# Duplicated keys, fewer threshold counts on one engine, and the value products of attention taken head by head

## The chip, the cores and the metric

The kernel runs on one core of a Trainium2 chip. The core has TensorE (PE; its weight loads are listed apart as PEld), VectorE (DVE), ScalarE (ACT), GpSimd (POOL) and SyncE (SP, which here only issues transfers). The metric is the device time of one execution in microseconds (us).

## The reference, cut to what matters

One layer of a hybrid encoder: 1024 prompt frames and 32 sample frames go through an input projection; its columns feed an indexer with sparse attention (eight query heads, four key/value heads) and an RWKV-7 recurrence; then an output projection and a squared-ReLU MLP follow.

```python
dots = jnp.einsum('bthd,bsd->bths', qi, ki_all) * (IDX_DIM ** -0.5)
score = jnp.einsum('bths,bth->bts', jax.nn.relu(dots), wi)
score = jnp.where(admissible[None], score, -jnp.inf)
_, idx = lax.top_k(score, topk)                       # topk = 256 for the prompt, 136 for the sample
...
s = jnp.einsum('btkgd,btskd->btkgs', qg, kg) * (HEAD_DIM ** -0.5)
p = jax.nn.softmax(jnp.where(valid[:, :, None, None, :], s, -jnp.inf), axis=-1)
o = jnp.einsum('btkgs,btskd->btkgd', p, vg)
...
y = h + jnp.square(jax.nn.relu(rms_norm(h) @ w_ff1)) @ w_ff2
```

## The kernel before

Frames go in nine tiles: t = 0 to 7 are 128 prompt frames each (tile t sees 128(t+1) keys), t = 8 is the 32 sample frames (544 keys). Products that need accuracy split an operand in a high part (F32R) and the remainder. The order of the instructions on each engine is laid down when the program is built: the code emits work in program order with priorities, and a planner with its own costs places it. So a line may run well ahead of or behind its place in the code.

**Index scores** (`idx_tile`, called for the tiles in the order 2, 3, 4, 5, 8, 6, 7). For each of eight index heads and each piece of up to 512 keys, line 324 multiplies the stacked query (high part on rows 0 to 63, remainder on rows 64 to 127) with the high part of the keys, which stands twice (`kiA`, 128 rows); line 325 adds the product of the high query with the remainder of the keys (`kiB`, 64 rows). ACT takes the relu (326), DVE weighs and sums (330). The projections of other tiles (209) run between them.

**Threshold search** (`topk`). The 256th largest score of each row is found bit by bit in 31 steps: count the scores below a candidate, then three small DVE instructions (365, 366, 368) set the next candidate. There are two groups of tiles (`SLS`). Group 0, tiles 2, 3, 4, 5, 8, counts on DVE (341). Group 1, tiles 6 and 7, counts on ACT (363), but in the first 15 steps (`i >= 16`) it too counts on DVE, since those steps of both groups read `S.upper`, copies of the upper halves of the scores as bf16, which ACT makes in `main2` (519). `norm_tile` calls and `zs_block` calls (three fills of 24 products of 352 columns in line 441, from which ACT writes `zm` and `tm`, 450 and 451; DVE copies two columns to `shl`, 446) each end with one step of both groups. PE has two buffers for these fills.

**Attention** (`attn_all`) and the **recurrence** (`rwkv_all`) run interleaved, as two generators; the recurrence has a front (with the triangular inverse, `lane_inverse`, DVE 832, 843 and POOL 837, 839) and a back per 256 frames. Attention goes through 36 items: four key/value heads j, and for each the nine tiles (8, 0, 1, 2, 3, 4, 5, 7, 6), two query heads per item. `prep` transposes the keys (1070) and splits them in `Ks` or `Kp`, with the high part on rows 0 to 63 and the remainder on rows 64 to 127; `query` puts the high query twice in `Q` (1093, 1094) and its remainder in `Ql` (1095, 64 rows). `scores` multiplies `Q` (1107, 128 rows) and `Ql` (1108, 64 rows). `turn` transposes the exponentials (1131). `product` multiplies 128 keys of values (64 features) with both heads' 256 columns at once (1146), output 64 features by 256; at the item's end it transposes the inverse sums by head (1151), multiplies (1153, 1154) and stores. After it come the output projection (1264) and the MLP (1328, 1348).

Of the kernel before, what the change touches and what calls it, by code (L numbers as in the profile page):

```python
# [150 lines left out]
def phase_a(S, pwx, pwy, pa, pi, px, xp, ps, late):  # L151
# [92 lines left out]
    S.upper = None  # L244
# [5 lines left out]
    kiB = pi.tile([64, 1024], F32R, name="kiB")  # L250
    ksA = pi.tile([128, 544], F32R, name="ksA")
    ksB = pi.tile([64, 544], F32R, name="ksB")
# [34 lines left out]
    def key_turn(t):  # L287
        r = rows_of(t)
        if t < 8:
            key_T(kiA, kiB, t * 128, KN.pop(t), r)  # L290
        else:
            key_T(ksA, ksB, 512, KN.pop(t), r)

    def cache_keys():
        for c in range(4):
            ck = pa.tile([128, 64], F32, name="ck", bufs=2)
            nc.sync.dma_start(ck, I["cache_kidx"][0, 0, c * 128:(c + 1) * 128])
            key_T(ksA, ksB, c * 128, ck, 128)

    def idx_tile(t, W):  # L300
        r = rows_of(t)
        z = pa.tile([128, 512], F32, name="zq", bufs=ZQB)[:r]
        proj_tok(z, t, W, 512)
        rope(z.rearrange("p (h d) -> p h d", h=8), t, 8)
        pt = ps.tile([128, 4, 128], F32, name="pt", bufs=2)
        for b in range(4):
            nc.tensor.transpose(pt[:, b, :r], z[:, b * 128:(b + 1) * 128], S.ident[:r, :r])
        qs = late["pj"].tile([128, 4, 2, 128], F32R, name="qs", bufs=2)
# [35 lines left out]
    def topk(X):  # L344
# [9 lines left out]
        for i in range(30, -1, -1):  # L354

            upper = i >= 16 and S.upper
            if X.exact or upper:
                count(X, ALU.is_lt, c_of, S.upper if upper else S.sc)
            else:
                for j, t in enumerate(X.SL):  # L360
                    r = rows_of(t)
                    n = S.sc[t].shape[1]
                    nc.scalar.activation(junk2[:r, :n], S.sc[t][:r, :n], AF.Sign, bias=c_of(j, r), scale=-1.0,
                                         accum_out=cnt[:r, j:j + 1])
            nc.vector.tensor_tensor(nac, cnt, X.off[:, 0] if X.exact or upper else X.off[:, 1], op=ALU.is_gt)
# [61 lines left out]
    def zs_block(i, W, o_, pool, mu1):  # L427
# [5 lines left out]
        for b, (o, n) in enumerate(TB):  # L433
# [78 lines left out]
    def main2():  # L512
        S.upper, c = {}, 0
        for X in TK:
            for t in X.SL:
                n = S.sc[t].shape[1]
                S.upper[t] = junk2 if t == 7 else S.eqb[:, c:c + n]
                c += n * (t != 7)
                (nc.gpsimd.tensor_copy if t in UPP else nc.scalar.copy)(S.upper[t][:rows_of(t), :n], S.sc[t][:rows_of(t)].bitcast(BF16)[:, 1:2 * n:2])
# [532 lines left out]
def attn_all(S, ap, ps):  # L1052
# [6 lines left out]
    def prep(j, samp):  # L1059
# [4 lines left out]
        A = ap.tile([128, n], F32R, name="K" + sx, bufs=1)  # L1064
        for t0 in range(0, nt, 4):
            t1 = min(nt, t0 + 4)
            p = ps.tile([128, 512], F32, name="ptr", bufs=PTB)
            for t in range(t0, t1):
                r = 32 if t == 4 and samp else 128
                nc.tensor.transpose(p[0:64, (t - t0) * 128:(t - t0) * 128 + r], kt[:r, t], S.ident[:r, :r])  # L1070
# [4 lines left out]
        J[j, samp] = A, vt  # L1075

    def query(k):
# [13 lines left out]
        w.Ql = Y = ap.tile([64, 2, 128], F32R, name="Ql", bufs=2)  # L1091
        src = p.rearrange("p (h q) -> p h q", h=2)[:, :, :r]
        nc.scalar.activation(X[0:64, :, :r], src, AF.Copy, scale=0.125)
        nc.scalar.activation(X[64:128, :, :r], src, AF.Copy, scale=0.125)
        nc.vector.scalar_tensor_tensor(Y[:, :, :r], src, 0.125, X[0:64, :, :r].bitcast(F32), op0=ALU.mult, op1=ALU.subtract)

    def scores(k, h):
# [3 lines left out]
        A = J[j, t == 8][0]  # L1101
        w.s[h] = s = ap.tile([128, 1024], F32, name="s", bufs=XPB)[:r, :n]
        m = w.m[:, h * 3:h * 3 + 2]
        for i, c0 in enumerate(range(0, n, 512)):
# [3 lines left out]
            nc.tensor.matmul(pd, w.Ql[:, h, :r], A[0:64, c0:c1], start=False, stop=True)  # L1108
# [26 lines left out]
    def product(k, g, nk, x, hi):  # L1135
# [3 lines left out]
        if g == 0:  # L1139
            w.pb = ps.tile([128, 512], F32, name="po", bufs=1)[0:64]  # L1140
            w.po = w.pb[:, 0:2 * r].rearrange("p (h q) -> p h q", h=2)
# [7 lines left out]
        p = w.pb[:, 256:256 + 2 * r].rearrange("p (h q) -> p h q", h=2)  # L1149
# [5 lines left out]
        nc.sync.dma_start(S.od[j * 128:j * 128 + 128, t * 128:t * 128 + r].rearrange("(h p) q -> p h q", h=2), t1)  # L1155
# [234 lines left out]
UPP = ()  # L1390
# [17 lines left out]
SLS = ((2,3,4,5,8),(6,7))  # L1408
# [11 lines left out]
def body(tc, I, O, dbg=None):  # L1420
# [4 lines left out]
    with pool(name="const") as cp, pool(name="dram", space=DRAM) as dp:  # L1425
# [18 lines left out]
        with pool(name="xnt") as xp, pool(name="psA", space=PSUM) as ps:  # L1444
# [16 lines left out]
            S.eqb = eq.rearrange("p a b -> p (a b)").bitcast(BF16)  # L1461
# [86 lines left out]
```

## Time and profile before

| | |
|---|---|
| time, three runs | 1846.62, 1850.66, 1853.6 us; median 1850.66 |
| profiled execution | 1847.36 us, span 1845.6 us |
| PE busy, share of the span | 1716.0 us, 93% |
| DVE, ACT, POOL busy | 986.4, 674.8, 587.0 us |
| chain that ended last | PE 66%, DVE 17%, POOL 6% |

A busy PE is modelled: products overlap, so busy time isn't the time that the products need. Where products follow each other without a wait, the distance from start to start tells that. The profile's chain is the work that ended last, followed back from the end; its shares tell which engine set the time of a stretch.

### The profile page before, as it was taken

Reading aid. Unit: us, or ns where it says so; the run is one execution under the profiler, and the core shown is the slowest. Engines: PE = TensorE matmul, PEld = TensorE weight load, DVE = VectorE, ACT = ScalarE, POOL = GpSimd, SP = SyncE. Lnnn points to the kernel's source line nnn. Section 1 sums busy time; section 2 is a strip of 40 time slices with the busy share of each in tenths; the row PEclk is TensorE's granted clock in tenths of the full one; section 3 lists DMA queues with packets and bytes.
Section 4 is the critical chain, followed back from the end, with each engine's and each line's share of the span. In section 5 each row is a group of like instructions: output and inputs, shape, how many; then the busy total and the mean of one; then the engine's idle time right before and its main releaser. Section 6 shows DMA issues by size and latency. Waiting matters only on the chain.

```text
span 1845.6 us, 29489 instructions
## 1 busy us (share of the span) xinstructions
PE 1716.0 (93%) x11394; PEld 1489.6 (81%) x11394; DVE 986.4 (53%) x2127; ACT 674.8 (37%) x1469; POOL 587.0 (32%) x894
## 2 busy tenths in 40 slices
PE   7999978798669988999899999999999999999999
PEld 6666667797546666666657779999999999999998
DVE  6456599999988777686552543222222222222224
ACT  6455432367635453454641332121212121212120
POOL 7446463244345434055210113121212131313120
PEclk9999988899658897999989999999999999999999
DMA  7111011132311112041212532111111111111105
GB/s 215 47 35 33 33 58 57 54 109 60 89 38 19 27 38 53 14 115 47 60 46 85 155 108 80 40 52 41 52 40 52 41 52 40 52 41 52 41 17 165
DMA packets 180196, 113.08 MB, mean 61 GB/s; under 512 B 51392, under 2 KB 169240, under 8 KB 180056
## 3 DMA queue, kind: packets, MB, share of 16 engines
q1 hardware_dynamic: 171224, 106.87, 20.6%
q10 hardware_dynamic: 8832, 4.33, 0.8%
q8 instruction: 89, 1.46, 0.3%
q14 instruction: 51, 0.42, 0.1%
HBM read 86.16 MB, written 25.01 MB: 60 GB/s over the span
## 4 chain that ended last, share of the span: by engine, by line
PE 66%; DVE 17%; POOL 6%; issue 3%; DMA 3%; ACT 3%; SPq 1%; DVEq 0%; POOLq 0%; ACTq 0%
PE pd L1328 20%; PE pr L1348 10%; DVE AR L341 7%; PE acc L209 5%; PE pc L1348 5%; PE po L1348 5%; PE po L1146 3%; POOL Yl L839 2%; POOL tl L837 2%; PE pd L325 2%; PE pd L1264 2%; PE ptr L1131 2%; DVE L L832 2%; PE pd L1108 1%; PE pd L324 1%
## 5 line engine op out<-in xcount | busy, mean ns | idle before, releaser
L1328 PE MATMUL pd<-hh,w1h 128*128 128x352 f32 x768 | 248.1, 323 | 2.4 <-issue 1.6
L1328 PE MATMUL pd<-hh,w1l 128*128 128x352 f32 x768 | 247.7, 323 | 0.7 <-DVE w1l L1195 0.7
L1328 PE MATMUL pd<-hl,w1h 128*128 128x352 f32 x768 | 247.0, 322 | 0.0
L1334 DVE TENSOR_TENSOR h2l<-rl,h2h 128x352 fp32r<-128x352 f32 x96 | 56.9, 593 | 275.7 <-ACT h2h L1333 275.7
L1332 POOL TENSOR_TENSOR rl<-rl 128x352 f32<-128x352 f32 x96 | 85.2, 888 | 214.0 <-ACT rl L1331 214.0
L1194 ACT CAST w2h<-w2r 128x512 fp32r<-128x512 f32 x64 | 39.7, 621 | 293.6 <-PE po L1348 144.7
L1328 PEld LDWEIGHTS pd<-hh,w1h 128*128 128x128 f32 x768 | 144.3, 188 | 3.0 <-issue 1.9
L1328 PEld LDWEIGHTS pd<-hh,w1l 128*128 128x128 f32 x768 | 144.3, 188 | 0.9 <-DVE w1l L1195 0.9
L1328 PEld LDWEIGHTS pd<-hl,w1h 128*128 128x128 f32 x768 | 144.9, 189 | 0.0
L1195 POOL TENSOR_TENSOR w2l<-w2r,w2h 128x512 fp32r<-128x512 f32 x32 | 41.6, 1299 | 299.8 <-ACT w2h L1194 289.3
L1348 PE MATMUL pr<-h2h,w2l 128*128 128x352 f32 x384 | 124.5, 324 | 0.0
L1348 PE MATMUL pr<-h2h,w2h 128*128 128x352 f32 x384 | 124.4, 324 | 0.0
L1348 PE MATMUL pr<-h2l,w2h 128*128 128x352 f32 x384 | 124.3, 324 | 0.0
L1354 DVE TENSOR_TENSOR ya<-ya,pr 128x352 f32<-128x352 f32 x84 | 43.8, 521 | 100.6 <-PE pr L1348 100.6
L1331 ACT ACTIVATE rl<-pd 128x352 f32<-128x352 f32 x96 | 44.3, 463 | 141.4 <-PE pd L1328 136.1
L1146 PE MATMUL po<-ph,vp 128*64 128x256 f32 x288 | 85.1, 418 | 2.1 <-DVE t L1154 1.6
L1131 PE MATMUL ptr<-ident,s 128*128 128x128 f32 (+2 forms) x328 | 66.6, 308 | 19.0 <-ACT s L1113 17.3
L837 POOL TENSOR_TENSOR tl<-L,Yl 128x56 f32<-128x56 f32 (+22 forms) x155 | 64.4, 416 | 61.6 <-DVE L L832 50.6
L341 DVE TENSOR_SCALAR_CACHE_REDUCE AR<-KB,cnd 128x384 bf16<-128x384 bf16 (+2 forms) x90 | 78.9, 877 | 1.2
L441 PE MATMUL acc<-xh,whx 128*128 128x352 f32 (+2 forms) x168 | 58.4, 348 | 19.3 <-ACT tm L451 12.0
L1333 ACT CAST h2h<-rl 128x352 fp32r<-128x352 f32 x96 | 46.6, 485 | 75.3 <-POOL rl L1332 75.3
L1131 PEld LDWEIGHTS ptr<-ident,s 128*128 128x128 f32 (+2 forms) x328 | 40.5, 155 | 39.9 <-ACT s L1113 18.8
(458 smaller groups left out, 4677.8 us busy)
## 6 DMA issues: line engine op xcount, KB each, us to landing
w1r<-in_w_ff_dram SPq DMA_DIRECT2D x32, 512.0 KB, 4.2
w2r<-in_w_ff_dram SPq DMA_DIRECT2D x64, 256.0 KB, 2.9
zsd<-zm SPq DMA_DIRECT2D x12, 528.0 KB, 3.0
wraw<-in_w_in_dram SPq DMA_DIRECT2D x24, 256.0 KB, 2.7
wraw<-in_w_in_dram SPq DMA_DIRECT2D x40, 128.0 KB, 2.5
x<-in_x_prompt_dram SPq DMA_DIRECT2D x8, 512.0 KB, 5.3
hres<-hd ACTq DMA_DIRECT2D x16, 256.0 KB, 3.0
out_dram<-hres SPq DMA_DIRECT2D x16, 256.0 KB, 2.4
```

The costliest lines, as they stand in the source:

```text
L209: nc.tensor.matmul(acc[:r, :n], l, w[:, :n], start=(i == 0), stop=(i == 23))
L341: nc.vector.tensor_scalar(junk[:r, :n], sc[t][:r, :n], get(j, r), None, op0=op, op1=ALU.add, accum_out=X.cnt[:r, j:j + 1])
L441: nc.tensor.matmul(acc[:m, :n], l, x, start=(j == 0), stop=(j == 23))
L837: eng.tensor_tensor(t_, L[:, 0:j, j:j + 1].to_broadcast([128, j, w]), Y[:, j:j + 1, m:16].to_broadcast([128, j, w]), op=ALU.mult)
L1131: nc.tensor.transpose(p[:x, i, h, :r], w.s[h][:, c0 + i * 128:c0 + i * 128 + x], S.ident[:r, :r])
L1146: nc.tensor.matmul(po, V[:x, kt], hi[:x, i, :, :r], start=(kt == 0), stop=(kt == w.nk - 1))
L1328: nc.tensor.matmul(acc, a[:, k], m[:, k, o:o + n], start=(i == 0), stop=(i == 23))
L1331: nc.scalar.activation(rl, acc, AF.Relu)
L1332: nc.gpsimd.tensor_tensor(rl, rl, rl, op=ALU.mult)
L1333: nc.scalar.copy(h2h[:, o:o + n], rl)
L1334: nc.vector.tensor_tensor(h2l[:, o:o + n], rl, h2h[:, o:o + n].bitcast(F32), op=ALU.subtract)
L1348: nc.tensor.matmul(acc, a[:, k], m[:, o:o + n], start=(i == 0), stop=(i == 11))
```

## The change

Keys and their remainders stand twice, on 128 rows, so that both products of a score use all rows of the array and the same stationary operand. `S.upper` and its copies go; group 0 loses tile 5 to group 1, and group 1 counts on ACT in all 31 steps. The `shl` copy goes from DVE to ACT. In `product`, each head has products of its own, 128 columns each, the first into output partitions 0 to 63 and the second into 64 to 127 (`PAR[h]`), so the output is 128 features by 128 queries, with one transpose, one copy, one multiplication and one plain store.

```diff
-    kiB = pi.tile([64, 1024], F32R, name="kiB")
+    kiB = pi.tile([128, 1024], F32R, name="kiB")
...
     def key_T(A, B, col, src, r):
-        nc.tensor.transpose(pt[:64, :r], src, S.ident[:r, :r])
-        nc.scalar.copy(A[0:64, col:col + r], pt[:64, :r])
-        nc.scalar.copy(A[64:128, col:col + r], pt[:64, :r])
-        nc.vector.tensor_tensor(B[:, col:col + r], pt[:64, :r], A[0:64, col:col + r].bitcast(F32), op=ALU.subtract)
+        nc.tensor.transpose(pt[:, :r], flat(src), S.ident[:r, :r])
+        nc.scalar.copy(A[:, col:col + r], pt[:, :r])
+        nc.vector.tensor_tensor(B[:, col:col + r], pt[:, :r], A[:, col:col + r].bitcast(F32), op=ALU.subtract)
...
     def key_turn(t):
+        k2 = pa.tile([128, 2, 64], F32, name="ck", bufs=2)[:r]
+        nc.gpsimd.tensor_copy(k2, KN.pop(t)[:, None, :].to_broadcast([r, 2, 64]))
...
     def cache_keys():
-            nc.sync.dma_start(ck, I["cache_kidx"][0, 0, c * 128:(c + 1) * 128])
+            for i in range(2):
+                nc.sync.dma_start(ck[:, i], I["cache_kidx"][0, 0, c * 128:(c + 1) * 128])
...
-                nc.tensor.matmul(o, qs[0:64, h // 2, h % 2, :r], B[:, c0:c1], start=False, stop=True)
+                nc.tensor.matmul(o, qs[:, h // 2, h % 2, :r], B[:, c0:c1], start=False, stop=True)
...
-            upper = i >= 16 and S.upper
-            if X.exact or upper:
-                count(X, ALU.is_lt, c_of, S.upper if upper else S.sc)
+            if X.exact:
+                count(X, ALU.is_lt, c_of, S.sc)
...
-                    nc.vector.tensor_copy(S.shl[:m, :, zc // 128 + (zc == 1600)], acc[:m, 319:352:32])
+                    nc.scalar.copy(S.shl[:m, :, zc // 128 + (zc == 1600)], acc[:m, 319:352:32])
...
-                (nc.gpsimd.tensor_copy if t in UPP else nc.scalar.copy)(S.upper[t][:rows_of(t), :n], S.sc[t][:rows_of(t)].bitcast(BF16)[:, 1:2 * n:2])
...
     def prep(j, samp):
-        A = ap.tile([128, n], F32R, name="K" + sx, bufs=1)
+        A, B = [ap.tile([128, 1024], F32R, name=x, bufs=1)[:, :n] for x in ("K", "Kl")]
...
+            k2 = ap.tile([128, 4, 2, 64], F32, name="k2", bufs=1)
+            nc.gpsimd.tensor_copy(k2[:r, :t1 - t0], kt[:r, t0:t1, None, :].to_broadcast([r, t1 - t0, 2, 64]))
...
-            nc.scalar.copy(A[0:64, c], p[0:64, :m])
-            nc.vector.tensor_tensor(A[64:128, c], p[0:64, :m], A[0:64, c].bitcast(F32), op=ALU.subtract)
+            nc.scalar.copy(A[:, c], p[:, :m])
+            nc.vector.tensor_tensor(B[:, c], p[:, :m], A[:, c].bitcast(F32), op=ALU.subtract)
...
     def query(k):
-        nc.scalar.activation(X[64:128, :, :r], src, AF.Copy, scale=0.125)
-        nc.vector.scalar_tensor_tensor(Y[:, :, :r], src, 0.125, X[0:64, :, :r].bitcast(F32), op0=ALU.mult, op1=ALU.subtract)
+        nc.vector.scalar_tensor_tensor(X[64:128, :, :r], src, 0.125, X[0:64, :, :r].bitcast(F32), op0=ALU.mult, op1=ALU.subtract)
...
-            nc.tensor.matmul(pd, w.Ql[:, h, :r], A[0:64, c0:c1], start=False, stop=True)
+            nc.tensor.matmul(pd, X[:, h, :r], B[:, c0:c1], start=False, stop=True)
...
     def product(k, g, nk, x, hi):
-            nc.tensor.matmul(po, V[:x, kt], hi[:x, i, :, :r], start=(kt == 0), stop=(kt == w.nk - 1))
+            for h in range(2):
+                nc.tensor.matmul(po[PAR[h]], V[:x, kt], hi[:x, i, h, :r], start=(kt == 0), stop=(kt == w.nk - 1))
...
-        for h in range(2):
-            nc.tensor.transpose(p[:, h], w.x[:, h], S.ident[:r, :r])
-        t1 = ap.tile([64, 2, 128], F32, name="t1", bufs=2)[:, :, :r]
+        nc.tensor.transpose(p, flat(w.x), S.ident[:r, :r])
+        t1 = ap.tile([128, 128], F32, name="t1", bufs=2)[:, :r]
...
-SLS = ((2,3,4,5,8),(6,7))
+SLS = ((2,3,4,8),(5,6,7))
```

## Rows read from the trace of the kernel before

**Rows 1.** Windows: length, busy us of PE, PEld, DVE, ACT, POOL; clock, DMA
```profile
80.00:228.00 148.00, 148.00 (x646) 97.67 (x645) 81.29 (x128) 72.04 (x157) 72.78 (x114) 1.00 0.11 31
228.00:520.00 292.00, 233.84 (x1257) 215.22 (x1255) 282.04 (x719) 147.66 (x306) 113.31 (x134) 0.86 0.24 68
520.00:870.00 350.00, 313.13 (x3127) 224.32 (x3128) 262.07 (x566) 166.05 (x411) 163.47 (x354) 0.86 0.18 42
870.00:1002.00 132.00, 123.00 (x930) 82.31 (x929) 62.72 (x176) 60.70 (x144) 18.03 (x21) 0.92 0.20 57
```

**Rows 2.** Chain that ended last, by line, of 80:228, 228:467, 520:870 and 870:1002
```profile
by line: PE acc L209 53.5%; PE pd L325 23.4%; PE pd L324 16.3%; PE acc L200 4.1%; PE pt L307 2.3%; ACT rl L326 0.4%; issue 0.0%
by line: DVE AR L341 52.9%; issue 10.8%; DVE cnd L366 5.5%; DVE nac L365 5.2%; DVE cnd L368 4.5%; DVE D L655 2.9%; POOL zm L453 2.1%; ACT AR L363 2.0%; DVE tmp L701 1.6%; DMA g<-in_g_dram 1.5%; DMA zsd<-zm 1.3%; DVE zq L421 1.3%; DVE cen L5
by line: POOL Yl L839 10.7%; POOL tl L837 10.6%; DVE L L832 9.0%; PE po L1146 8.1%; issue 6.9%; PE ptr L1131 4.9%; DVE G L843 4.4%; PE pd L1108 3.9%; PE pr L720 3.9%; PE pd L1107 3.3%; DVE G L723 2.2%; PE pr L798 1.9%; PE pc L896 1.6%; POOL
by line: PE po L1146 21.4%; PE pr L1264 14.0%; PE ptr L1131 12.0%; PE pd L1108 8.0%; PE pd L1107 5.7%; DMA AR<-od 3.4%; ACT G L1230 3.1%; PE po L1151 2.6%; PE pr L814 2.3%; ACT s L1113 2.2%; PE pr L958 2.1%; PE pc L896 1.9%; PE pc L884 1.9%
```

**Rows 3.** Timeline of PE in the index stage: start, duration, line, form
```profile
197.15 0.40 PE L324 MATMUL pd<-kiA,qs 128*128 128x512 f32 x1
197.48 0.49 PE L325 MATMUL pd<-kiB,qs 64*128 64x512 f32 x1
197.90 0.44 PE L324 MATMUL pd<-kiA,qs 128*128 128x384 f32 x1
...
199.21 0.40 PE L209 MATMUL acc<-wly,xh 128*128 128x512 f32 x1
199.45 0.40 PE L209 MATMUL acc<-why,xl 128*128 128x512 f32 x1
```

**Rows 4.** Waits: the load engine before 64-row products, 80:228 and 500:1002
```profile
PEld pd L325 <- issue: 21.2, 74, 0.4
PEld pd L1108 <- issue: 13.2, 50, 0.4
```

**Rows 5.** Groups by form: busy us, mean ns of one count | idle before
```profile
L341 DVE TENSOR_SCALAR_CACHE_REDUCE AR<-KB,cnd 128x768 bf16<-128x768 bf16 x15 | 15.2, 1011 | 0.6
L341 DVE TENSOR_SCALAR_CACHE_REDUCE AR<-G,cnd 128x768 bf16<-128x768 f32 x16 | 16.2, 1010 | 0.3
L341 DVE TENSOR_SCALAR_CACHE_REDUCE AR<-KB,cnd 128x896 bf16<-128x896 bf16 x15 | 17.0, 1136 | 0.0
L341 DVE TENSOR_SCALAR_CACHE_REDUCE AR<-AR,cnd 128x1024 bf16<-128x1024 bf16 x15 | 19.1, 1273 | 0.0
L363 ACT ACTIVATE AR<-G,cnd 128x1024 bf16<-128x1024 f32 x16 | 18.4, 1150 | 0.3
```

**Rows 6.** Timeline of DVE: the same count in two steps of the search
```profile
300.69 1.13 DVE L341 TENSOR_SCALAR_CACHE_REDUCE AR<-KB,cnd 128x896 bf16<-128x896 bf16 x1
...
307.72 1.14 DVE L341 TENSOR_SCALAR_CACHE_REDUCE AR<-KB,cnd 128x896 bf16<-128x896 bf16 x1
```

**Rows 7.** Waits in 228:400: us in total, times, longest
```profile
ACT zm L450 <- DVE shl L446: 41.7, 5, 11.7
...
PE acc L441 <- ACT tm L451: 19.9, 9, 6.1
```

**Rows 8.** Timeline of PE in the attention stage
```profile
703.33 0.69 PE L914 MATMUL pc<-G,VU 128*64 128x64 f32 x16
...
707.72 0.63 PE L758 MATMUL pr<-ident,v 128*64 128x128 f32 x4
708.27 1.94 PE L1146 MATMUL po<-ph,vp 128*64 128x256 f32 x8
```

**Rows 9.** Groups by form: a value product, its load, a POOL copy
```profile
L1146 PE MATMUL po<-ph,vp 128*64 128x256 f32 x288 | 85.1, 418 | 2.1 <-DVE t L1154 1.6 <-DVE ph L1132 0.5
L1146 PEld LDWEIGHTS po<-ph,vp 128*64 128x64 f32 x288 | 35.2, 144 | 29.5 <-issue 14.2 <-DVE t L1154 1.8 <-DVE ph L1132 0.7
L1119 POOL COPY x<-m 128x128 f32<-128x128 f32 x32 | 11.3, 352 | 119.1 <-DVE m L1117 96.7 <-DVE y L977 10.7 <-PE po L1151 7.0
```

More of the change, by code (lines that the diff above doesn't have):

```diff
@@ L243, in phase_a @@
         X.off = S.tk.tile([128, 2, len(SL)], F32, name="off" + str(len(SL)))
-    S.upper = None
     ones = S.tk.tile([128, 1], F32, name="ones")
@@ L249, in phase_a @@
     kiA = pi.tile([128, 1024], F32R, name="kiA")
-    kiB = pi.tile([64, 1024], F32R, name="kiB")
+    kiB = pi.tile([128, 1024], F32R, name="kiB")
     ksA = pi.tile([128, 544], F32R, name="ksA")
-    ksB = pi.tile([64, 544], F32R, name="ksB")
+    ksB = pi.tile([128, 544], F32R, name="ksB")
     KN = {}
@@ L288, in key_turn @@
         r = rows_of(t)
+        k2 = pa.tile([128, 2, 64], F32, name="ck", bufs=2)[:r]
+        nc.gpsimd.tensor_copy(k2, KN.pop(t)[:, None, :].to_broadcast([r, 2, 64]))
         if t < 8:
-            key_T(kiA, kiB, t * 128, KN.pop(t), r)
+            key_T(kiA, kiB, t * 128, k2, r)
         else:
-            key_T(ksA, ksB, 512, KN.pop(t), r)
+            key_T(ksA, ksB, 512, k2, r)
     def cache_keys():
         for c in range(4):
-            ck = pa.tile([128, 64], F32, name="ck", bufs=2)
-            nc.sync.dma_start(ck, I["cache_kidx"][0, 0, c * 128:(c + 1) * 128])
+            ck = pa.tile([128, 2, 64], F32, name="ck", bufs=2)
+            for i in range(2):
+                nc.sync.dma_start(ck[:, i], I["cache_kidx"][0, 0, c * 128:(c + 1) * 128])
             key_T(ksA, ksB, c * 128, ck, 128)
@@ L364, in topk @@
                                          accum_out=cnt[:r, j:j + 1])
-            nc.vector.tensor_tensor(nac, cnt, X.off[:, 0] if X.exact or upper else X.off[:, 1], op=ALU.is_gt)
+            nc.vector.tensor_tensor(nac, cnt, X.off[:, 0] if X.exact else X.off[:, 1], op=ALU.is_gt)
             nc.vector.scalar_tensor_tensor(cnd, nac, i, cnd, op0=ALU.logical_shift_left, op1=ALU.bitwise_xor)
@@ L512, in main2 @@
     def main2():
[L513 to L518, printed above, removed]
-                (nc.gpsimd.tensor_copy if t in UPP else nc.scalar.copy)(S.upper[t][:rows_of(t), :n], S.sc[t][:rows_of(t)].bitcast(BF16)[:, 1:2 * n:2])
         nc.gpsimd.memset(S.shl, 0.0)
@@ L1067, in prep @@
             p = ps.tile([128, 512], F32, name="ptr", bufs=PTB)
+            r = 32 if t0 == 4 and samp else 128
+            k2 = ap.tile([128, 4, 2, 64], F32, name="k2", bufs=1)
+            nc.gpsimd.tensor_copy(k2[:r, :t1 - t0], kt[:r, t0:t1, None, :].to_broadcast([r, t1 - t0, 2, 64]))
             for t in range(t0, t1):
-                r = 32 if t == 4 and samp else 128
-                nc.tensor.transpose(p[0:64, (t - t0) * 128:(t - t0) * 128 + r], kt[:r, t], S.ident[:r, :r])
+                nc.tensor.transpose(p[:, (t - t0) * 128:(t - t0) * 128 + r], flat(k2[:r, t - t0]), S.ident[:r, :r])
             m = 32 if t1 == 5 else 512
             c = slice(t0 * 128, t0 * 128 + m)
-            nc.scalar.copy(A[0:64, c], p[0:64, :m])
-            nc.vector.tensor_tensor(A[64:128, c], p[0:64, :m], A[0:64, c].bitcast(F32), op=ALU.subtract)
-        J[j, samp] = A, vt
+            nc.scalar.copy(A[:, c], p[:, :m])
+            nc.vector.tensor_tensor(B[:, c], p[:, :m], A[:, c].bitcast(F32), op=ALU.subtract)
+        J[j, samp] = A, vt, B
     def query(k):
@@ L1090, in query @@
         w.Q = X = ap.tile([128, 2, 128], F32R, name="Q", bufs=2)
-        w.Ql = Y = ap.tile([64, 2, 128], F32R, name="Ql", bufs=2)
         src = p.rearrange("p (h q) -> p h q", h=2)[:, :, :r]
         nc.scalar.activation(X[0:64, :, :r], src, AF.Copy, scale=0.125)
-        nc.scalar.activation(X[64:128, :, :r], src, AF.Copy, scale=0.125)
-        nc.vector.scalar_tensor_tensor(Y[:, :, :r], src, 0.125, X[0:64, :, :r].bitcast(F32), op0=ALU.mult, op1=ALU.subtract)
+        nc.vector.scalar_tensor_tensor(X[64:128, :, :r], src, 0.125, X[0:64, :, :r].bitcast(F32), op0=ALU.mult, op1=ALU.subtract)
     def scores(k, h):
@@ L1100, in scores @@
         r, n, X = w.r, w.n, w.Q
-        A = J[j, t == 8][0]
+        A, _, B = J[j, t == 8]
         w.s[h] = s = ap.tile([128, 1024], F32, name="s", bufs=XPB)[:r, :n]
@@ L1139, in product @@
         if g == 0:
-            w.pb = ps.tile([128, 512], F32, name="po", bufs=1)[0:64]
-            w.po = w.pb[:, 0:2 * r].rearrange("p (h q) -> p h q", h=2)
+            w.pb = ps.tile([128, 512], F32, name="po", bufs=1)
+            w.po = w.pb[:, 0:r]
         po = w.po
@@ L1145, in product @@
             kt = g * 2 + i
-            nc.tensor.matmul(po, V[:x, kt], hi[:x, i, :, :r], start=(kt == 0), stop=(kt == w.nk - 1))
+            for h in range(2):
+                nc.tensor.matmul(po[PAR[h]], V[:x, kt], hi[:x, i, h, :r], start=(kt == 0), stop=(kt == w.nk - 1))
         if kt < w.nk - 1:
             return
-        p = w.pb[:, 256:256 + 2 * r].rearrange("p (h q) -> p h q", h=2)
-        for h in range(2):
-            nc.tensor.transpose(p[:, h], w.x[:, h], S.ident[:r, :r])
-        t1 = ap.tile([64, 2, 128], F32, name="t1", bufs=2)[:, :, :r]
+        p = w.pb[:, 256:256 + r]
+        nc.tensor.transpose(p, flat(w.x), S.ident[:r, :r])
+        t1 = ap.tile([128, 128], F32, name="t1", bufs=2)[:, :r]
         nc.scalar.copy(t1, p)
         nc.vector.tensor_tensor(t1, t1, po, op=ALU.mult)
-        nc.sync.dma_start(S.od[j * 128:j * 128 + 128, t * 128:t * 128 + r].rearrange("(h p) q -> p h q", h=2), t1)
+        nc.sync.dma_start(S.od[j * 128:j * 128 + 128, t * 128:t * 128 + r], t1)
         del W[k]
@@ L1389 @@
 FOFF = -100
-UPP = ()
 EARLY = 0
@@ L1460, in body @@
             S.eq = [eq[:, i] for i in range(2)]
-            S.eqb = eq.rearrange("p a b -> p (a b)").bitcast(BF16)
             with pool(name="pq", side="right") as pq:
```

## The prediction

> **What bounds the kernel now.** I read the windows first, then the chain by stretch, then for each stretch the rows of the lines that change. Four stretches are touched; the output projection and the MLP behind them are not.
>
> In 80:228, the index scores, PE is busy all the time at full clock [rows 1], and the chain is PE alone [rows 2]: lines 209, 325 and 324. In 228:520, the threshold search with the recurrence's last inputs, DVE is busy 282.0 of 292 us, PE 233.8 at a clock of 0.86, ACT 147.7 [rows 1]; in the chain up to 467, DVE's counts alone are 52.9% [rows 2]. PE and ACT lag because of DVE: ACT waited 41.7 us for five `shl` copies that stood behind counts in DVE's queue, and PE then waited for ACT's `tm`, 19.9 us in nine waits [rows 7]. In 520:870 the chain alternates: the triangular inverse on POOL and DVE (10.7, 10.6, 9.0 and 4.4%) and PE's attention lines [rows 2]. In 870:1002 it is mostly PE, with line 1146 at 21.4% [rows 2].
>
> **Index scores.** Two products of 512 columns that use the same rows follow each other at 199.45 − 199.21 = 0.24 us. The 128-row product of a score takes 197.48 − 197.15 = 0.33 to the next start, the 64-row product 197.90 − 197.48 = 0.42 [rows 3]. So going into the 64-row form costs 0.09 and out of it 0.18, in sum 0.28 a visit; the load engine stood 74 times before such a product [rows 4]. The change lets both use 128 rows: 74 x 0.28 = 21 us. From the other side, the chain has 23.4% of 148 = 34.6 us in line 325 and 24.1 in 324 [rows 2]; 43% of the one and 27% of the other is again 21. Upper bound 27, if each exit also delays the next product by 0.09; lower bound 12, if DVE (81.3 of 148) and ACT (72.0) [rows 1] with their turns take over for the last, long tiles. I take 21, since PE has nothing else to wait for there. The nine POOL copies of keys (0.35 us each by the nearest copy [rows 9]) and four more 32 KB loads in SP's queue hide behind PE: POOL is busy 72.8 of 148 and DMA 0.11 [rows 1]; without that cover the copies would cost 3 us. ACT saves one copy a key tile, on no path.
>
> **Threshold search.** Dropping the bf16 copies makes no count slower: 768 scores take 1011 ns from bf16 and 1010 from f32 [rows 5]. The Trainium skill (VectorE: DVE Perf Modes, "The perf-mode tier table (the rule you actually need)") gives a tensor_scalar twice the rate on bf16 that it has on fp32; by it group 0 would lose up to 15 x 4 x 0.5 = 30 us, an estimate from that page and tile 5's row, and this stretch would gain 16 in place of 46. This trace doesn't agree for this counting form, so nothing is lost.
>
> DVE loses tile 5, 31 x 1.01 = 31.3 us, and in 15 steps tiles 6 and 7, 15 x (1.136 + 1.273) = 36.1 [rows 5]. Tile 5's final refinement comes back on DVE, two passes that I bound by 1 and 3 us together and take as 2. Net 65: DVE goes from 282 to 217. One step took 307.72 − 300.69 = 7.03 us of DVE [rows 6]; it becomes about 4. ACT gains tile 5 for 31 steps, 0.86 to 1.15 us each (1.150 for 1024 scores [rows 5], scaled or not), 27 to 36, taken as 29, and tiles 6 and 7 for 15 steps, at most 15 x 2 x 1.15 = 34; seven bf16 copies go (about 0.8 us each by their size against a count). ACT: 147.7 + 29 + 34 − 5, about 205. So no engine needs over 217, or 234 for PE by its busy time, which was partly slow-clocked. DVE alone ran at 97%; now a step hops between ACT and DVE, ACT also empties PE's fills, and DVE would be at 88% in 246 us. I take 246: a gain of 46. Bounds: 65, where DVE stays packed, and 15, where the hops eat the rest. Moving `shl` costs ACT 14 tiny copies but ends the wait of [rows 7] on DVE; what is late next is PE's fill behind a count on ACT (the rival below).
>
> **Attention.** Eight value products of 256 columns took 1.94 us, the last 0.42 of it its own length [rows 8, 9]: 0.217 a product, 0.85 ns a column. By head it is two of 128 columns, 0.11 each (four such in line 758 span 0.63 [rows 8]). Do two of them on different halves run side by side? Line 914 is the nearest row: 128 rows by 64 columns, alternating halves, 16 in 0.69, or 0.03 each after the first's 0.23, where 64 columns at 0.85 ns are 0.054 [rows 8]. They do. So the pair costs 0.11, and the 288 products [rows 9] go from 62.5 to 31.7 us, −31. (The sample's 40 are too short to gain.) Each product has its own load, so loads double; line 914 also loads before each product and keeps its 0.03.
>
> Scores: 50 visits to the 64-row form [rows 4] x 0.28 = 14. One transpose of sums fewer in 36 items x 0.11 = 4. That is 49 us of PE work. What of it lies on the chain: line 1146 has 8.1% of 350 and 21.4% of 132, 28.4 and 28.2 us, of which half goes; 1108 has 13.7 and 10.6, 1107 has 11.6 and 7.5, of which 43% and 27% go [rows 2]; with the transposes 23 us in 520:870 and 23 in 870:1002. In the first the inverse (34.7% of 350 = 121 us) doesn't shrink and becomes the chain where PE gets short, so I take half, 11; in the second 19. Sum 30, bounds 12 and 49. ACT and DVE save the second `Q` copy and half the length of 1153 and 1154; they hide behind PE, as before.
>
> What is added: per key/value head, three POOL copies of 512 columns and one of 128, in all 12 and 4. At 0.352 for 128 [rows 9] they cost 5.6 us if length didn't matter and 18 if it did; I take 18 on POOL. They stand in its queue before or behind the inverse's 62 instructions a unit, and `k2` has one buffer, so the second copy of a `prep` waits for four transposes. POOL is busy 163 of 350 [rows 1], but 21% of the chain is POOL. Sample and prompt now share one buffer each of `K` and `Kl`, so new keys wait for the last scores of the item before, up to 7 x 1 us. I add 5 for both, bounds 0 and 25.
>
> **Sum.** −21 − 46 − 30 + 5 = −92, from the profiled execution's 1847.4 (its span is 1845.6) to 1755. The median of the runs lies 3.3 higher: 1758.
>
> **Rivals.** *ACT slows the search, still faster.* The three counts, 3.1 us of ACT a step, take turns with DVE's queue so that a step stays at 6 to 7 us. For it: both engines need over 200 us in the stretch. Against: 31 steps of about 5 us (3.1 of counts, DVE's small ones, two hand-overs) are 155. Gain 15 there: 1789.
>
> *PE's fills starve; slower.* ACT must empty a fill before PE may use its buffer again, and now stands up to 3.1 us in counts, each held by DVE's candidate. If all 42 fills waited a whole round, 42 x 3.15 = 132 us on PE's 234: the stretch takes 366, 74 more than now, and with −46 elsewhere the kernel 28 more: 1879. It decides from (292 + 46 − 234) / 42 = 2.5 us a fill. For it: in [rows 7] PE's waits are all on `tm`, of 2.2 us each. Against: there were nine of them, most of that time behind DVE's `shl`, which goes.
>
> *The halves don't pair.* Then 576 products of 0.11 are what 288 of 0.217 were, the value term is nothing, and the sum −73: 1777. If besides each load (0.144 [rows 9]) stood bare, PE would get 83 us more work, two thirds of it on the chain: 1832. Line 914 speaks against both, and line 1146 itself, whose 0.217 leaves no room for a bare load. The Trainium skill (TensorE: Matmul & The Clock Gate, "Part 3: Packing small matmuls — row/col tiling") says that loads overlap running products only where their row groups differ; both halves use all rows, so by it the bare load would hold. No row here agrees.
>
> *The recurrence sets the end.* Its inverse and back go on at their own pace and attention's 30 shrink to 5: 1783.
>
> **Chances.** The sum as it stands 0.70, within 1725 to 1790; ACT slows the search 0.12; the recurrence 0.06; the halves 0.05; starved fills 0.07, of which 0.04 beyond the point where it gets slower and 0.03 near it. So faster 0.93, same 0.03, slower 0.04, where 0.5%, 9 us, is about what a measurement of this kernel can tell from no change. The terms' bounds together would be 1710 to 1837; as they won't all fall on one side, the range that leaves out 2 in 10 is 1715 to 1805.
>
> **What would show it.** After the change, 324 and 325 should follow each other at 0.24; the index stage end some 20 us sooner; 341 have no bf16 inputs and 134 counts in place of 194 (counted in the code: 31 x 4 + 7 + 3 for 15 x 7 + 16 x 5 + 7 + 2); ACT have 363 with three sizes; the stretch from the last relu (326) to the first exponential be some 45 us shorter; 1146 show 576 products of 128 columns, in pairs 0.11 apart; attention's last product come some 90 us before 1000. I am wrong if PE waits long for `tm` with ACT in 363, if line 1146's instructions stand 0.11 apart one by one, or if lines 837 and 839 fill the chain while PE idles.

## The result and the profile after

The kernel after takes 1795.95 us (median of four runs, 1791.09 to 1798.12; before 1848.64 beside it), a ratio of 0.9712 with an interval of 0.9676 to 0.9747. That is faster, inside the range, but 53 us faster where 92 were forecast. The profiled execution took 1798.12 us, its span is 1796.3 us. Line numbers have shifted: 324, 325 and 326 are 325, 326 and 327 now, 341 is 342, 363 is 362, 441 is 440, 451 is 450, 977 is 969, 1113 is 1105, 1146 is 1139, 1264 is 1256.

The windows of the kernel after, cut where its stages now end, with the columns of [rows 1]:

```profile
80.00:200.00 120.00, 117.16 (x653) 98.48 (x652) 83.54 (x129) 69.22 (x158) 84.24 (x110) 1.00 0.13 36
200.00:450.00 250.00, 212.69 (x1217) 200.39 (x1215) 202.93 (x540) 189.06 (x405) 121.69 (x142) 0.90 0.28 80
450.00:850.00 400.00, 338.64 (x3416) 263.89 (x3416) 290.97 (x630) 176.27 (x426) 170.17 (x359) 0.76 0.16 37
850.00:931.00 81.00, 74.33 (x872) 57.50 (x871) 52.89 (x145) 47.47 (x121) 21.10 (x30) 0.94 0.29 80
931.00:1038.00 107.00, 105.82 (x496) 84.57 (x497) 45.41 (x77) 25.30 (x48) 6.73 (x9) 1.00 0.38 118
```

The index stage takes 120 us where it took 148. The search stretch has no full engine left: DVE 203 of 250, ACT 189. The stage with attention and the recurrence begins 57 us sooner (by its first exponential, below), but its first 400 us run at a granted clock of 0.76, and behind it the projection stands alone for 107 us.

PE's timeline in the index stage, to be held against [rows 3]:

```profile
173.24 0.40 PE L325 MATMUL pd<-kiA,qs 128*128 128x512 f32 x1
173.48 0.39 PE L326 MATMUL pd<-kiB,qs 128*128 128x512 f32 x1
173.71 0.34 PE L325 MATMUL pd<-kiA,qs 128*128 128x384 f32 x1
173.88 0.34 PE L326 MATMUL pd<-kiB,qs 128*128 128x384 f32 x1
```

The starts are 0.24 and 0.23 apart where they were 0.33 and 0.42. The groups of the relu line, before and after in two fences, give its first and last start:

```profile
L326 ACT ACTIVATE rl<-pd x96: 170/587/602, 84.7 to 227.5; 128x512 f32<-128x512 f32 x48, 128x384 f32<-128x384 f32 x16, 128x128 f32<-128x128 f32 x8, 128x256 f32<-128x256 f32 x8
```
```profile
L327 ACT ACTIVATE rl<-pd x96: 167/586/612, 86.0 to 200.2; 128x512 f32<-128x512 f32 x48, 128x384 f32<-128x384 f32 x16, 128x128 f32<-128x128 f32 x8, 128x256 f32<-128x256 f32 x8
```

So the stage ends 27.3 us sooner. There are 96 relus (x96), one for each pair of products 325 and 326. For the search, four groups of the kernel after, counts on ACT (362) and on DVE (342), the masks (404) and the exponentials (1105):

```profile
L362 ACT ACTIVATE AR<-G,cnd x93: 917/1042/1177, 208.7 to 456.9; 128x768 bf16<-128x768 f32 x31, 128x896 bf16<-128x896 f32 x31, 128x1024 bf16<-128x1024 f32 x31
...
L342 DVE TENSOR_SCALAR_CACHE_REDUCE AR<-G,cnd x65: 861/884/1262, 209.8 to 482.6; 128x640 bf16<-128x640 f32 x31, 32x664 bf16<-32x664 f32 x31, 128x768 bf16<-128x768 f32 x1, 128x896 bf16<-128x896 f32 x1
...
L404 ACT ACTIVATE mb<-KB x7: 507/737/1057, 391.3 to 506.4; 128x384 bf16<-128x384 f32 x1, 128x512 bf16<-128x512 f32 x1, 128x640 bf16<-128x640 f32 x1, 32x544 bf16<-32x544 f32 x1
...
L1105 ACT ACTIVATE s<-s,m x72: 385/747/1158, 453.9 to 925.1; 32x544 f32<-32x544 f32 x8, 128x128 f32<-128x128 f32 x8, 128x256 f32<-128x256 f32 x8, 128x384 f32<-128x384 f32 x8
```

The same two lines of the kernel before, where the masks are line 405 and the exponentials 1113:

```profile
L405 ACT ACTIVATE mb<-KB x7: 523/739/1056, 474.5 to 518.3; 128x384 bf16<-128x384 f32 x1, 128x512 bf16<-128x512 f32 x1, 128x640 bf16<-128x640 f32 x1, 128x768 bf16<-128x768 f32 x1
...
L1113 ACT ACTIVATE s<-s,m x72: 386/748/1153, 510.7 to 980.3; 32x544 f32<-32x544 f32 x8, 128x128 f32<-128x128 f32 x8, 128x256 f32<-128x256 f32 x8, 128x384 f32<-128x384 f32 x8
```

The first exponential comes 56.8 us sooner, but the last mask only 11.9. Group 1's 31 steps take 248 us (208.7 to 456.9), about 8 each, where I had forecast 5. The waits of 200:450 say why:

```profile
ACT AR L362 <- DVE cnd L367: 36.8, 18, 9.3
...
PEld acc L440 <- ACT tm L450: 19.7, 10, 8.2
DVE nac L364 <- ACT AR L362: 17.5, 13, 4.7
PE acc L440 <- ACT tm L450: 16.8, 10, 7.9
```

ACT waits 36.8 us for DVE's candidates, DVE 17.5 us for ACT's counts, and between its counts, which take it some 105 us, ACT is busy with fills, weights and the recurrence's front: 189 us busy and 37 waiting in 250. PE's wait for `tm` is 16.8 us in ten waits; over the same stretch of both kernels, 200:520, it was 27.9 in 13 before.

The tile `KB` of the search is also unit 1's scratch in the recurrence. Its groups in 480:560 (masks 397 to 404, recurrence 681):

```profile
L403 DVE SCALAR_TENSOR_TENSOR KB<-KB,need,G x3: 1069/1341/1442, 496.0 to 504.9; 128x768 f32<-128x768 f32 x1, 128x896 f32<-128x896 f32 x1, 128x1024 f32<-128x1024 f32 x1
L404 ACT ACTIVATE mb<-KB x3: 845/950/1057, 497.1 to 506.4; 128x768 bf16<-128x768 f32 x1, 128x896 bf16<-128x896 f32 x1, 128x1024 bf16<-128x1024 f32 x1
L681 DVE TENSOR_TENSOR KB<-k,D x2: 1219/1220/1222, 516.4 to 518.7; 64x1024 f32<-64x1024 f32 x2
```

Unit 1 writes `KB` only behind the last mask, as both stand in one tile. But in this kernel the mask is not what held the write: the last mask ended at 507.4 us, and the write came 9.0 us later. In between DVE, whose queue the write stands in, waited for POOL's inverse of unit 0 (`Yl`, 831):

```profile
509.98 4.54 DVE L835 STREAM_TRANSPOSE G<-Yl 32x512 f32<-32x512 f32 x4 [3.66 <-POOL Yl L831]
...
516.35 1.22 DVE L681 TENSOR_TENSOR KB<-k,D 64x1024 f32<-64x1024 f32 x1
```

And the end of the stage, the timeline around 933 us:

```profile
930.61 0.33 PE L1143 MATMUL po<-ident,x 128*128 128x128 f32 x1
...
932.76 0.51 DVE L969 TENSOR_TENSOR y<-y,pr 128x64 f32<-128x64 f32 x2
933.03 0.19 PEld L1256 LDWEIGHTS pr<-G 128*128 128x128 f32 x1
933.03 0.49 PE L1256 MATMUL pr<-G 128*128 128x512 f32 x1
```

Attention's last product and the recurrence's last step (line 969) are 2 us apart, and the projection begins as the recurrence ends. In the kernel before the projection also began as the recurrence ended (at 969 us), but attention still ran to 1000, and the two overlapped.

Last the value products. PE's timeline shows 16 of 128 columns in two places, against eight of 256 in 1.94 [rows 8]; under each stand windows of it, the first of all of PE, the second of line 1139 alone (length, busy us of PE, in the second of PEld too, granted clock, DMA):

```profile
525.18 1.98 PE L1139 MATMUL po<-ph,vp 128*64 128x128 f32 x16
```
```profile
525.18:527.09 1.91, 1.91 (x17) 0.50 0.00 0
```
```profile
565.49 1.30 PE L1139 MATMUL po<-ph,vp 128*64 128x128 f32 x16
```
```profile
565.48:565.97 0.49, 0.48 (x4) 0.48 (x6) 0.51 0.00 0
565.97:566.62 0.65, 0.65 (x15) 0.58 (x12) 1.00 0.00 0
```

At 565 the first two pairs ran at a granted clock of 0.51, the lower level of 1.2 GHz, in 0.49 us, the other six at 2.4 GHz in 0.65, or 0.11 a pair (three of the 15 products counted there reach over the cut). So the halves do pair. At 525 all 16 ran at 1.2 GHz and took as long as eight wide ones had at full clock.

### The profile page after: what moved, and what is told of

It reads as the page before. It is cut to its first block, busy times and chain, and to the rows that moved or that the text cites. A ratio compares the mean times of both kernels' runs of the same rounds, so it can differ in the third digit from the quotient of the medians.

```text
span 1796.3 us, 30013 instructions
## 1 busy us (share of the span) xinstructions
PE 1663.9 (93%) x11686; PEld 1509.2 (84%) x11686; DVE 936.1 (52%) x1996; ACT 707.6 (39%) x1549; POOL 618.6 (34%) x919
## 4 chain that ended last, share of the span: by engine, by line
PE 63%; DVE 12%; ACT 5%; POOL 4%; issue 3%; DMA 2%; SPq 0%; DVEq 0%; ACTq 0%; POOLq 0%
PE pd L1320 20%; PE pr L1340 10%; PE pc L1340 5%; PE po L1340 5%; PE pd L1256 3%; PE po L1139 2%; DVE AR L342 2%; ACT AR L362 2%; PE ptr L1123 2%; PE pr L1256 2%; PE acc L440 2%; DVE L L824 1%; PE pr L712 1%; POOL tl L829 1%; POOL Yl L831 1%
## 5 line engine op out<-in xcount | busy, mean ns | idle before, releaser
L362 ACT ACTIVATE AR<-G,cnd 128x768 bf16<-128x768 f32 (+2 forms) x93 | 96.7, 1040 | 42.2 <-DVE cnd L367 36.8
L1105 ACT ACTIVATE s<-s,m 32x544 f32<-32x544 f32 (+8 forms) x72 | 55.4, 770 | 74.8 <-DVE m L1102 74.6
L1340 PEld LDWEIGHTS pr<-h2l,w2h 128*128 128x128 f32 x384 | 72.3, 188 | 0.1
L1340 PEld LDWEIGHTS pr<-h2h,w2h 128*128 128x128 f32 x384 | 72.2, 188 | 0.1
```

What stands on the lines that cost most here:

```text
L1105: nc.scalar.activation(s, s, AF.Exp, bias=m[:, i:i + 1], scale=-1.0, accum_out=w.m[:, 6 + h:7 + h])
L1340: nc.tensor.matmul(acc, a[:, k], m[:, o:o + n], start=(i == 0), stop=(i == 11))
```

## The experiments

Each ratio is to the kernel before on the same chip, with its 95% interval.

| run | ratio | median us |
|---|---|---|
| index_alone | 0.986 (0.9801 to 0.9918) | 1828.02 |
| search_alone | 0.9986 (0.996 to 1.0013) | 1849.49 |
| attention_alone | 0.9851 (0.9807 to 0.9895) | 1824.17 |
| attention_wide | 0.9968 (0.9939 to 0.9997) | 1848.03 |
| wide_values | 0.9664 (0.963 to 0.9698) | 1790.67 |
| after_again | 0.9694 (0.9646 to 0.9742) | 1797.86 |
| same_half | 0.976 (0.9711 to 0.9809) | 1810.11 |
| both_on_halves | 0.983 (0.9779 to 0.9881) | 1823.89 |
| after_off100 | 0.9737 (0.9681 to 0.9793) | 1804.67 |
| wide_off100 | 0.9724 (0.9671 to 0.9777) | 1803.91 |
| wide_tail | 0.9807 (0.9749 to 0.9866) | 1818.63 |
| wide_tile5 | 0.9689 (0.9631 to 0.9746) | 1798.78 |

**The three parts, each put alone into the kernel before.**

```diff
# index_alone: key_T, key_turn, cache_keys, and in idx_tile
-                nc.tensor.matmul(o, qs[0:64, h // 2, h % 2, :r], B[:, c0:c1], ...)
+                nc.tensor.matmul(o, qs[:, h // 2, h % 2, :r], B[:, c0:c1], ...)
# search_alone: no S.upper, shl on ACT, and
-SLS = ((2,3,4,5,8),(6,7))
+SLS = ((2,3,4,8),(5,6,7))
# attention_alone: prep, query, scores, product as after
```

> Only the index part of the change (keys on all 128 rows, both products of a score in the same form); search and attention as before. Theory L (the gain of the whole was cut by what sets the end later: group 1's counts on ACT hold the masks back, unit 1's recurrence waits for their scratch, and attention then ends together with the recurrence): the index stage ends 27 us sooner, as in the kernel after, and as nothing behind it is changed the whole is 22 to 27 us shorter than before. Rival C (a lower granted clock behind the stage gives part back): the stage ends 27 us sooner, but the whole gains 15 or less.

> Only the search's part of the change (no bf16 copies, tile 5 counted on ACT, shl emptied by ACT); index scores and attention as before. Theory L: the first exponential comes about 29 us sooner, the masks of group 1 only some 10 us sooner or not at all, unit 1's part of the recurrence hardly sooner, so the whole gains 0 to 15 us. Rival S (the stretch's gain goes through to the end, and what ate the sum lies in attention): 25 to 30 us.

> Only attention's part of the change (keys on 128 rows, both score products in one form, value products by head); index scores and search as before. Theory L: attention's last product comes down to the recurrence's end at 968 us (32 us sooner), and as the projection's early products no longer overlap attention's tail, some 19 of it are given back: the whole gains 10 to 20 us. Rival A (the POOL copies of keys and the shared buffers of K eat the gain): the recurrence or attention itself gets longer, gain 0 to 8. My forecast's terms would give 25.

By the ratios they gave 26, 2.6 and 27.6 us of 1854.41; their sum, 56, is within the intervals what the whole change gave (53). Index met theory L, attention came above it and at my own forecast's 25. The search gave nothing that can be told from zero. The groups of search_alone, masks (403) and exponentials (1104):

```profile
L403 ACT ACTIVATE mb<-KB x7: 567/732/1057, 411.9 to 540.7; 128x384 bf16<-128x384 f32 x1, 128x512 bf16<-128x512 f32 x1, 128x640 bf16<-128x640 f32 x1, 32x544 bf16<-32x544 f32 x1
```
```profile
L1104 ACT ACTIVATE s<-s,m x72: 384/743/1152, 470.8 to 959.2; 32x544 f32<-32x544 f32 x8, 128x128 f32<-128x128 f32 x8, 128x256 f32<-128x256 f32 x8, 128x384 f32<-128x384 f32 x8
```

The first exponential came 40 us sooner than before (470.8 for 510.7), which is near the 46 of my sum, but the last mask 22 us later (540.7 for 518.3), and the recurrence's last step 10 us later (978.1 for 967.6). In the kernel after, the last mask is likewise 17 us later than with the index part alone (506.4 for 489.1).

Unit 1's first write of `KB` tells what the later mask did. In the kernel before it stands at 537.3 us and with the index part alone at 508.1, both times 17.9 us behind the end of the last mask, so something else held it there. In search_alone it stands at 541.8, just as the last mask ends: the mask had used up these 18 us and 4.5 more.

**What the end hangs on.** For every kernel, from the groups of these lines: the last start of the recurrence's last step and of a value product, the first start of the projection, and the span (us):

```
kernel           recurrence  value  projection  span    span - projection
before           967.6      1000.0  969.4       1845.6  876.2
index_alone      958.4       972.4  958.8       1824.8  866.0
search_alone     978.1       968.3  977.5       1843.5  866.0
attention_alone  960.1       972.6  960.4       1824.1  863.7
attention_wide   992.7      1006.7  993.1       1859.9  866.8
after            933.0       930.4  933.0       1796.3  863.3
after_again      932.6       929.9  932.6       1795.9  863.3
wide_values      928.6       907.2  919.4       1786.2  866.8
same_half        942.7       940.0  942.8       1807.7  864.9
both_on_halves   959.2       948.6  957.8       1822.1  864.3
after_off100     951.2       948.5  951.2       1813.7  862.5
wide_off100      934.4       932.8  934.2       1797.5  863.3
wide_tail        950.0       964.1  950.4       1817.5  867.1
wide_tile5       927.5       956.3  928.7       1802.2  873.5
```

In 13 of 14 the projection begins within 2 us of the recurrence's last step, in wide_values 9 us ahead of it, though in some kernels attention had ended 9 to 12 us before and in others it ran on for 12 to 31. The rest is then 862 to 867 us; only where attention runs on by 28 or 31 us does it cost another 7 to 10. So the time of the whole goes with the recurrence's end and not with attention's, and in the kernel before attention's tail of 31 us cost 10 more. That the one sets the other is argued from this table and not shown. The rival is PE's own work: the recurrence's products, attention's and the projection's stand in one queue in the planner's order, PE is busy for 92 to 94% of the span in all 14 runs, and in 850:931 of the kernel after for 74 of 81 us; it may be what carries both.

**The value products undone.** First the kernel after with the one wide product; then attention_wide, the kernel before with the score part of attention's change alone.

```diff
# wide_values, against after (with its po, t1 and store as before)
-            for h in range(2):
-                nc.tensor.matmul(po[PAR[h]], V[:x, kt], hi[:x, i, h, :r], ...)
+            nc.tensor.matmul(po, V[:x, kt], hi[:x, i, :, :r], ...)
# attention_wide: before, with prep, query and scores as after
```

> The kernel after with its value products as before: 256 columns for both heads on one half, two transposes of sums. Theory L: attention ends with the recurrence either way, so the whole stays within 12 us of the kernel after. Rival V (the value products lie on the chain): 18 to 25 us slower than the kernel after, since PE's time in that line goes from 68 back to 91 us.

> The kernel before with only the score part of attention's change (keys and queries on 128 rows, no switch of form), value products wide as before. With products by head as well that change gave 27.6 us (ratio 0.9851). If the score forms carry it all, this gives 25 to 35 us (0.981 to 0.9865); if the value products by head carry half, as in my sum, this gives 8 to 15 us (0.992 to 0.996).

wide_values was not slower than the kernel after but 5 to 7 us faster by the medians, though the intervals overlap (0.963 to 0.9698 against 0.9676 to 0.9747 and 0.9646 to 0.9742). So rival V fell, and my value term with it. In the kernel before the same products by head are worth 21.7 us (27.6 less 5.9 for the score part), by the two intervals give or take some 10. The score part gave 5.9, below what I had put down for the case that the products carry half (8 to 15); the profiled execution of attention_wide lies 13.7 us above its median, so its rows in the table count as the high end.

The value products' windows in 450:931 (line 1139, in wide_values 1138) and the whole stage's in 550:900, for after and then for wide_values:

```profile
450.00:931.00 481.00, 68.25 (x656) 41.83 (x656) 0.79 0.19 44
...
550.00:900.00 350.00, 319.51 (x3524) 249.16 (x3524) 242.68 (x542) 161.72 (x410) 142.26 (x308) 0.83 0.20 48
```
```profile
450.00:931.00 481.00, 90.09 (x328) 39.31 (x328) 0.87 0.20 49
...
550.00:900.00 350.00, 322.70 (x3471) 234.78 (x3470) 258.52 (x579) 177.38 (x432) 145.66 (x312) 0.95 0.20 48
```

The products by head do take 22 us less of PE, but PE is granted 0.83 of its clock in 550:900 where it had 0.95 with wide ones: 0.12 of 350 is 42 us of full clock. How much of that the time felt isn't shown.

**Is it the halves?** Two kernels take the pair apart:

```diff
# same_half: both heads into partitions 0 to 63
+                nc.tensor.matmul(po[:, h], V[:x, kt], hi[:x, i, h, :r], start=(kt == 0 and h == 0), ...)
# both_on_halves: each half gets both heads' 256 columns
+                nc.tensor.matmul(po[PAR[h]], V[:x, kt], hi[:x, i, :, :r], ...)
```

> The kernel after with 576 value products of 128 columns, one a head, but both heads on the same half of the array, output as 64 features by two heads as before. In the run before, wide products ended attention 23 us sooner than products by head, at a granted clock of 0.95 against 0.83 in 550:900. Theory K (side by side on two halves the products leave PE short of streaming, and the granted clock falls): here they stand 0.11 apart one by one, the clock in 550:900 is near 0.95, and the time is within 10 us of the kernel with wide products (some 1785 to 1800, ratio 0.963 to 0.972). Rival N (the number of products and loads costs, not their place): as slow as the kernel after or up to 30 us slower, with the clock as low as there.

> The kernel after with twice the columns: each half of the array gets the queries of both heads (256 columns), and the half that belongs to the other head is dropped, so PE streams as long as with wide products but in pairs on both halves, with as many products and loads as after. Theory K: the clock in 550:900 comes back to about 0.95, and in spite of the doubled columns the time is the same as after or less, 1785 to 1797. Rival P (the halves themselves lower the clock, or the doubled loads do): the clock stays near 0.83 and the time is 10 to 25 us over that of the kernel after.

> The kernel after, once more, beside the three others on the same chip. If products by head are slower than wide ones for good, it is again at 0.970 to 0.974 of the kernel before with a clock of 0.80 to 0.86 in 550:900; if the first pair of runs differed by chance, its clock and time come out as with wide products (0.966, 0.95).

The kernel after came out as the first time (1797.86 us, the same 0.83). Theory K fell in both: with one half the clock came to 0.88 and the time was 12 us longer than after_again, with wide products on both halves the clock was 0.86 and the time 26 us longer. Rivals N and P, which lay the cost on the number of products and loads, fit the times, but not the clocks, which came out between. All of these kernels also differ in how the planner placed the rest, so I put one number of the planner in both forms:

```diff
-OFF = -200
+OFF = -100
```

> The kernel after with one number of the planner changed: the recurrence stands 100 behind attention in the order instead of 200. Products by head as after. Theory R (the end of the recurrence sets the end of the whole): the recurrence ends 5 to 20 us sooner and the whole with it (1777 to 1793), and the whole minus the recurrence's end stays 863 to 867. Rival Q (PE's sum of work sets it, whatever the order): both within 5 us of the kernel after. Beside the next one it also shows what another order of the same work is worth.

> The same number changed in the kernel with wide value products: with the one before, a second pair of kernels that differ in the value products alone. If products by head cost time in themselves, this one is again 5 to 12 us faster than its pair; if the first pair's difference came from how the planner put the rest in order, the sign is open and the difference may be anything from -10 to +10. My forecast's value term (31 us of PE work) would make this one 15 to 30 us slower than its pair.

The pair's difference is gone: 1804.67 by head, 1803.91 wide, at clocks of 0.80 and 0.89 in 550:900. Theory R's constant held (862.5 and 863.3), but the recurrence ended 18 and 6 us later with the other number, not sooner (the profiled execution of after_off100 lies 10.8 us above its median, so its 18 is the high end). So the products by head were worth 21.7 us in one surrounding, and in the two others nothing that can be told from zero (-5 to -7 and -1). Their clock over the whole span, which every run has, was the lower one in two pairs: 0.925 to 0.930 against 0.948 and 0.949, and 0.919 to 0.926 against 0.933 to 0.939. In the pair around the kernel before the runs overlap (0.933 to 0.942 against 0.934 to 0.949; 0.82 and 0.84 in 550:900).

**The search again.** Two tries to bring group 1's masks forward, on top of wide_values:

```diff
# wide_tail: the last 11 steps of group 1 on DVE
-            if X.exact:
+            if X.exact or i < 11:
# wide_tile5: tile 5 back on DVE
-SLS = ((2,3,4,8),(5,6,7))
+SLS = ((2,3,4,5,8),(6,7))
```

> The kernel after with wide value products, and with the last 11 of group 1's 31 steps counted on DVE, which stands free by then (group 0 is through at 374 us in the kernel after, group 1 at 458). Theory L (group 1's counts on ACT, 8.2 us a step, hold back the masks, and those hold back the recurrence and attention): counts end some 40 us sooner, the masks of group 1 too, the first exponential 10 to 15 us sooner (the fills end at 416 and are next), and the whole is 15 to 40 us shorter than with wide products alone: 1750 to 1775, ratio 0.945 to 0.958. Rival F (the end is set by fills, attention and recurrence behind them, not by the masks): within 6 us of wide products alone, 0.9664.

> The kernel after with wide value products and the old split of the search (tiles 2, 3, 4, 5, 8 on DVE, 6 and 7 on ACT), still without bf16 copies. So far the projection starts as the recurrence ends, and the whole is that moment plus 863 to 867 us. Theory M (the recurrence waits for group 1's masks, which come late because three ACT counts a step take 8 us): with two counts the step falls to some 7 us, the masks end at 470 to 490 instead of 506, the recurrence ends 15 to 30 us sooner, and the whole comes to 1760 to 1778 (ratio 0.950 to 0.959). Rival D (DVE is the bound of the search again): masks end no sooner, within 6 us of wide products alone (0.9664) or up to 20 us slower.

wide_tail went the other way. ACT's counts ended at 349 us, but group 1's steps then stood among group 0's in DVE's queue, DVE waited 19.3 us for ACT's counts ("nac") in 320:540, group 0's first mask came at 491 for 390 and the last at 533 for 505. The recurrence ended 21 us later, and the whole was 28 us slower than wide_values. wide_tile5 brought the last mask to 496 (forecast 470 to 490), but the recurrence ended only 1 us sooner, the first exponential came 26 us later, and attention ran 28 us past the projection's start: 8 us slower. In both kernels unit 1's write of `KB` now follows the last mask at once (534.0 and 497.3 us, for 514.9 in wide_values), and DVE is seen to wait for it; the line is wide_tail's, in 320:540:

```profile
DVE KB L681 <- ACT mb L404: 0.4, 1, 0.4
```

So a late mask does hold unit 1's scratch back. But in wide_tile5 this write came 18 us sooner than in wide_values and the recurrence's end only 1 us: neither the masks nor this scratch set that end there. That the later masks are what made wide_tail's recurrence end 21 us later fits, but isn't shown, as the whole order differs.

## Why the prediction was right and wrong

- **Direction, range.** Faster, within 1715 to 1805, as forecast at 0.93; the size was 53 of 92. The sum itself, to which I had given 0.70 within 1725 to 1790, did not hold: 1795.95 lies outside. That the time fell in the range owes to the room left for the rivals and partly to luck: index came out above its term, which hid a part of what search lacked.
- **Index scores, right.** 0.24 between 325 and 326, the stage 27 us shorter (forecast 21, bound 27), 26 us alone. The 21 was too small for a reason that the rows show: I had counted the 74 waits of the load engine as the visits to the 64-row form, but each of the 96 pairs of products was one (96 relus), and 96 x 0.28 is 27. (My 0.09 and 0.18 add up to 0.27, but from the pair's start to the next product's it is 0.75 in [rows 3] and 0.47 after, 173.71 − 173.24, so 0.28 holds.) The costs that I called hidden stayed hidden: PE was busy for 117 of the stage's 120 us.
- **Threshold search, the step that failed.** "I take 246: a gain of 46" (bounds 15 to 65). Alone it gave 2.6 (interval -2.4 to 7.4), below my lower bound (the whole change without it was not run). The sum of busy times was not far off: the first exponential did come 29 us sooner beyond the index stage's 27. But I took that moment as the end of the stretch. The recurrence's unit 1 can't write its scratch before the last mask of group 1, and group 1, now with three tiles and no help from DVE, takes 8 us a step and ends its masks 17 to 22 us later than without this edit. So this write came 4.5 us later in search_alone than in the kernel before, held by the mask, and 8 us later in the kernel after (516.4) than with the index part alone (508.1), there behind POOL's inverse. That the gain was gone by this write is shown; what keeps it from coming back behind the write is open. The rival "ACT slows the search" had the mechanism, with steps of 6 to 7 us and a price of 31 against the sum; it did not have this consequence.
- **Attention, size right alone, not separable in the whole.** 27.6 alone against 30 less 5, of which 21.7 lay in the value products. The halves pair as forecast, 0.11 at full clock. The Trainium skill (TensorE: Matmul & The Clock Gate, "Part 3: Packing small matmuls — row/col tiling") says that loads overlap running products only where their row groups differ, by which the loads would stand bare; these rows don't agree. PE's busy time in the value products fell by 22.5 us (90.7 to 68.25), not 31; the 31 was worked out from the distances of starts at full clock within a run of products, and what made up the rest isn't shown. But beside the other edits the value term is nothing: without it they give 62 us (wide_values), though by their own runs they are 34 (26, 2.6 and 5.9), and with it 53 to 57. So the parts don't add, and that their sum came near the whole proves none of them. The POOL copies and shared key buffers (+5) were not taken apart.
- **The recurrence sets the end, the rival that I gave 0.06.** The table above fits it in every kernel, without showing that PE's own work isn't behind both. I had given it a price of 25 us by the pace of the inverse and back, and let attention's gain reach the end otherwise. The last product did come 70 us sooner (930.4 for 1000.0, forecast some 90), but the projection's first only 36, with the recurrence's last step (933.0 for 967.6). The rest of the 49 us between the spans, 13, is the tail that no longer stands behind it (863.3 for 876.2).
- **Fills starve: no.** PE waited 16.8 us for `tm`, over 42 fills 0.4 each against the 2.5 a fill at which it would have decided.
- **Open.** What sets the recurrence's end itself, its own chain on POOL and DVE or its share of PE; and why the clock is lower with products by head in two of three pairs. No run here takes either apart from the planner's new order.

wide_values was the fastest version: 0.9664 against 0.9694 and 0.9712 for the kernel after. Its runs (1788.24 to 1791.26) lie below or at the edge of the others (1791.09 to 1798.58), the intervals overlap, and a change of one planner number undid the difference.

## What to carry to other kernels

Ask what the next stage waits for (here a scratch tile that two users share, and an inverse on POOL), and count a gain there, not at the first instruction of that stage. Count a cost by the instructions that pay it, not by the waits that the profile happens to show. Moving work to an engine with room makes its own chain longer: follow the last result through that engine's queue, not the busy sums. Where a planner re-places everything, an edit's worth has to be taken in more than one surrounding before it is believed; here the same edit was worth 22 us in one and nothing in two others.

## What the hardware showed that I had not expected

Taking 22 us of PE's work out of a stage left PE with a lower granted clock in two pairs of kernels (0.83 for 0.95 and 0.80 for 0.89 in 550:900, and in every run of each pair over the whole span); in a third pair (0.82 for 0.84) the runs overlap. The kernels of a pair also differ in the planner's order, so the cause is open. In 450:520 of the kernel after, PE is busy for 35.16 of 70 us, and the granted clock is 0.52, nearly all at the lower level: this is the stretch in which attention has begun and group 1's masks, until 506 us, are still missing. A run of 16 products takes 1.30 us where the clock rises within it and 1.98 where it doesn't.
